# Thirty-two more bytes behind each of the six split-weight buffers of a two-layer hybrid trunk

## The chip, the core and the metric

The kernel runs on one core of one Trainium2 chip, in one launch. The metric is the device time of that launch in microseconds (us), the median of several runs. The core has a matrix engine (PE, with its weight loads listed apart as PEld), a vector engine (DVE), a scalar engine (ACT), GpSimd (POOL) and a queue engine (SP) that issues most of the transfers from device memory. Everything the engines read lies in the on-chip memory, which has 128 partitions; a tile takes the same bytes in every partition, and when this text gives an address, it is the byte within a partition.

## The reference

The program computes two layers of a decoder trunk on a 512 x 1024 sequence. Each layer is a half-weighted SwiGLU block, a mixer, and another half-weighted SwiGLU block, each on RMS-normalised input:

```python
x = x + 0.5 * swiglu(rmsnorm(x, g1), wg1, wu1, wd1)     # 1024 -> 2816 -> 1024
h = rmsnorm(x, gm)
z = h @ w_in                                            # columns go to three head groups
y = concat(s5_mixer(z...), hgrn2_mixer(z...), nsa_mixer(z...))
x = x + y @ w_out
x = x + 0.5 * swiglu(rmsnorm(x, g2), wg2, wu2, wd2)
```

A last normalisation closes the trunk. All inputs and weights are float32. Most of the arithmetic is in the dense products with `w_gate`, `w_up`, `w_down`, `w_in` and `w_out`.

## The kernel before

**Split products.** Activations are kept transposed (features on the partitions, the 512 tokens along the free axis). A float32 product is made of three products in the matrix engine's float32r type. Each operand is split into a rounded part and the rest: `whi` and `wlo` for the weights, and two halves each of `xs` (normalised input), `hb` (the hidden layer of the SwiGLU block) and `y` (mixer outputs) for the activations. `mm3` (lines 222 to 226) issues the three: L224 is `whi` by the rounded activation, L225 `whi` by the rest, L226 `wlo` by the rounded activation. In each of them a 128 x 128 block of weights is loaded and 512 token columns are streamed past it.

**The weights' way.** `wraw` (line 205) lets SP fetch up to 1024 columns of weights into one of four raw buffers. `wsplit` (line 212) takes one buffer named `whi` and one named `wlo` from pool `wp`, lets ACT round the raw weights into `whi` (L218), and lets DVE subtract to get `wlo` (L219). The pool has three buffers for each of the two names, so six in all. `dense_x` (line 228) uses a set for one output tile with eight 128-wide blocks; `ffn` (line 268) uses sets of 6 and 5 blocks for the down projection; `wout` (line 1353) uses sets of 4 blocks. `dense_tok` (line 1231, matmuls at L1250 to L1252) turns the roles round: there `xs` is loaded as the weight and 256 or 280 columns of `whi` or `wlo` are streamed. With 280 columns the slices of one buffer begin at columns 0, 280 and 560, which is byte 0, 1120 and 2240, or 0, 96 and 192 bytes past a multiple of 512.

**The order.** In the SwiGLU blocks the order is a plain loop, with small parameter work (`params`, line 378 on) woven in between. In the mixer a cooperative scheduler (`Weave`, line 38) interleaves generators for the dense projections and for the three head groups by weights and claimed costs that are written in the code. No address plays a part in either.

**Addresses.** The pools are opened in the constructor in a fixed order: `res`, `sm`, `al`, `big`, `wp`, and tiles are laid out in the order of their first use. `al` holds one unused tile of `ALIGN` = 192 bytes, behind which `x` begins at byte 24576, `xs` at 40960 and the raw weights at 73728, all multiples of 512. In the built program `whi` stands at 94208, 98304 and 102400, `wlo` at 106496, 110592 and 114688, each 4096 bytes long. Behind them stand `sq` (118784) and `rbc` (122880), and then the pools that come and go: the SwiGLU blocks' (`hb` at 129024, `ft`, `ft2`), the mixer's pool `mp` of 46 equal tiles of 2048 bytes from 126976 on, and the parameter pools. Tiles of the parameter pools do not begin at multiples of 512: `shm` and `Rs`, used by the matmuls of L703 and L704, begin 192 bytes past one in one layer and 480 past one in the other, and so do `cbw` and `cbt` of L717.

Of the kernel before, what the change touches and what calls it, by code (L numbers as in the profile page):

```python
# [11 lines left out]
F32R = mybir.dt.float32r  # L12
# [50 lines left out]
class Trunk:  # L63
# [147 lines left out]

    def wsplit(self, w, n, parts=1):
        nc = self.nc
        h = self.wp.tile([128, 1024], F32R, tag="whi", name="whi")
        lo = self.wp.tile([128, 1024], F32R, tag="wlo", name="wlo")
        for i in range(parts):
            sl = slice(i * n // parts, (i + 1) * n // parts)
            nc.scalar.copy(h[:, sl], w[:, sl])  # L218
            self.mark = nc.vector.tensor_tensor(lo[:, sl], w[:, sl], h[:, sl].bitcast(F32), op=OP.subtract)  # L219
        return h, lo  # L220
# [1277 lines left out]
```

## Time and profile before

| | |
|---|---|
| median of 3 runs | 2116.76 us (2115.8 to 2119.16) |
| the profiled execution, own time | 2116.3 us |
| its span, first to last instruction | 2114.5 us |
| PE busy | 2091.4 us, 99% of the span, 11192 matmuls |
| PEld busy (overlaps PE) | 1695.1 us, 80% |
| DVE busy | 1188.1 us, 56% |
| ACT busy | 786.7 us, 37% |
| POOL busy | 82.8 us, 4% |
| granted TensorE clock, mean | 0.996 of full speed |
| moved by DMA | 209.11 MB, 99 GB/s over the span |

The busy time of an engine is the time in which at least one of its instructions is shown as running. Matmuls are pipelined, so that one is shown for longer than it holds up the next: the pace of a stream of them is read from the distance between their starts. A group of instructions shows its busy time, the mean duration of one, and behind the second bar how long its engine was idle before it and what ended most of that. The chain of work that ended last is followed back from the last instruction, at each step to what released it.

### The profile page before, as it was taken

The page shows a single profiled execution, that of the slowest core. Times are in us where ns is not written, and L with a number is a line of the kernel's source. Part 1 is how long each engine was busy: PE and PEld are TensorE (multiplying, and loading weights), DVE is VectorE, ACT ScalarE, POOL GpSimd, SP SyncE. Part 2 cuts the span into 40 slices and gives each one's busy share as a digit, 9 for nine tenths or more (in the row PEclk, how much of TensorE's full clock was granted, in tenths as well). Part 3 has the DMA queues.
Part 4 walks back from the last instruction along what each step waited for, and adds up shares of the span by engine and source line. Part 5 has one row for each costly group of instructions (what it writes and reads, how often), then busy time and mean ns, then how long its engine had stood idle before and what let it go on. Part 6 is the DMA issues. An engine that isn't in the chain of part 4 may idle for free.

```text
span 2114.5 us, 28943 instructions
## 1 busy us (share of the span) xinstructions
PE 2091.4 (99%) x11192; PEld 1695.1 (80%) x11192; DVE 1188.1 (56%) x2653; ACT 786.7 (37%) x1455; POOL 82.8 (4%) x153
## 2 busy tenths in 40 slices
PE   8999999999999999999999999999999999999997
PEld 7888888877767888888888888888777678888886
DVE  7864545676765874543544343456777664334435
ACT  5322223445565432232332222243455663222321
POOL 1000000111000100000000000001100000000000
PEclk9999999999999999999999999999999999999999
DMA  5334433433101433432333233234321023333322
GB/s 193 112 104 128 138 127 104 139 113 101 51 16 43 149 117 95 150 97 81 109 100 94 83 114 100 75 115 138 110 75 51 26 80 90 87 93 113 97 82 68
DMA packets 69753, 209.11 MB, mean 99 GB/s; under 512 B 9272, under 2 KB 11912, under 8 KB 69616
## 3 DMA queue, kind: packets, MB, share of 16 engines
q1 hardware_dynamic: 58192, 172.19, 27.1%
q0 software_dynamic: 11280, 35.05, 4.8%
q8 instruction: 88, 1.44, 0.3%
q14 instruction: 49, 0.40, 0.1%
q10 hardware_dynamic: 144, 0.03, 0.0%
HBM read 194.63 MB, written 15.22 MB: 99 GB/s over the span
## 4 chain that ended last, share of the span: by engine, by line
PE 98%; DVE 1%; issue 0%; DMA 0%; ACT 0%; SPq 0%; POOL 0%; DVEq 0%; POOLq 0%
PE pd L224 28%; PE pd L226 27%; PE pd L225 27%; PE pno L1198 2%; PE ppt L1182 2%; PE psS L1159 2%; PE psS L1156 1%; PE plv L875 1%; PE pd L1250 1%; PE pd L1251 1%; PE pd L1252 1%; PE psc L1095 1%; PE pho L945 0%; PE pno L1201 0%; PE pY L784 0%
## 5 line engine op out<-in xcount | busy, mean ns | idle before, releaser
L218 ACT CAST whi<-wraw 128x1024 fp32r<-128x1024 f32 (+5 forms) x377 | 345.4, 917 | 1017.1 <-PE pd L225 703.6
L224 PE MATMUL pd<-xs,whi 128*128 128x512 f32 x1664 | 657.8, 395 | 6.7 <-ACT whi L218 6.1
L226 PE MATMUL pd<-xs,wlo 128*128 128x512 f32 x1664 | 652.2, 392 | 0.0
L225 PE MATMUL pd<-xs,whi 128*128 128x512 f32 x1664 | 650.8, 391 | 0.0
L219 DVE TENSOR_TENSOR wlo<-wraw,whi 128x1024 fp32r<-128x1024 f32 (+5 forms) x377 | 397.0, 1055 | 144.7 <-ACT whi L218 136.1
L224 PEld LDWEIGHTS pd<-xs,whi 128*128 128x128 f32 x1664 | 313.7, 188 | 76.1 <-ACT whi L218 6.1
L226 PEld LDWEIGHTS pd<-xs,wlo 128*128 128x128 f32 x1664 | 313.3, 188 | 66.6 <-issue 0.4
L225 PEld LDWEIGHTS pd<-xs,whi 128*128 128x128 f32 x1664 | 313.6, 188 | 64.1 <-DVE xs L164 1.0
L224 PE MATMUL pd<-hb,whi 128*128 128x512 f32 x682 | 265.8, 390 | 0.0
L226 PE MATMUL pd<-hb,wlo 128*128 128x512 f32 x682 | 265.4, 389 | 0.0
L225 PE MATMUL pd<-hb,whi 128*128 128x512 f32 x682 | 265.4, 389 | 0.0
L293 DVE TENSOR_TENSOR ft<-ft,pd 128x512 f32<-128x512 f32 x88 | 60.5, 687 | 247.5 <-PE pd L226 247.1
L287 DVE TENSOR_TENSOR ft<-pd,rbc 128x512 f32<-128x512 f32 x88 | 60.7, 690 | 189.0 <-PE pd L226 189.0
L226 PEld LDWEIGHTS pd<-hb,wlo 128*128 128x128 f32 x682 | 128.0, 188 | 26.8
L224 PEld LDWEIGHTS pd<-hb,whi 128*128 128x128 f32 x682 | 128.0, 188 | 26.3
L225 PEld LDWEIGHTS pd<-hb,whi 128*128 128x128 f32 x682 | 128.0, 188 | 26.3
L312 DVE TENSOR_TENSOR ft<-pd,r 128x512 f32<-128x512 f32 x62 | 42.9, 692 | 109.3 <-PE pd L226 109.1
L1166 ACT ACTIVATE P<-P,mx 128x128 f32<-128x128 f32 (+3 forms) x128 | 71.7, 561 | 51.9 <-DVE mx L1162 50.5
L1162 DVE CUSTOM_DVE_ANT_0 P<-Tb,psS 128x128 f32<-128x128 f32 (+3 forms) x128 | 60.7, 485 | 49.5 <-PE psS L1159 48.9
L295 DVE TENSOR_TENSOR hb<-ft,hb 128x512 fp32r<-128x512 f32 x88 | 60.3, 685 | 0.0
L288 ACT ACTIVATE ft<-ft 128x512 f32<-128x512 f32 x88 | 55.1, 627 | 13.1 <-DVE ft L287 12.8
L294 ACT CAST hb<-ft 128x512 fp32r<-128x512 f32 x88 | 54.8, 622 | 13.7 <-DVE ft L293 11.8
(388 smaller groups left out, 2158.3 us busy)
## 6 DMA issues: line engine op xcount, KB each, us to landing
wraw<-in_gu SPq DMA_DIRECT2D x175, 512.0 KB, 3.6
wraw<-in_dn SPq DMA_DIRECT2D x64, 384.0 KB, 3.1
wraw<-in_dn SPq DMA_DIRECT2D x64, 320.0 KB, 2.8
wraw<-in_win SPq DMA_DIRECT2D x32, 512.0 KB, 3.5
w<-sp POOLq DMA_DIRECT2D x32, 256.0 KB, 5.8
wraw<-in_wo SPq DMA_DIRECT2D x32, 256.0 KB, 2.6
Tb<-tbl POOLq DMA_DIRECT2D x16, 256.0 KB, 3.6
tbl<-ext POOLq DMA_DIRECT2D x1, 2560.0 KB, 19.7
```

The lines of the kernel that those rows point to most:

```text
L218: nc.scalar.copy(h[:, sl], w[:, sl])
L219: self.mark = nc.vector.tensor_tensor(lo[:, sl], w[:, sl], h[:, sl].bitcast(F32), op=OP.subtract)
L224: nc.tensor.matmul(ps, wh, xh, start=first, stop=False)
L225: nc.tensor.matmul(ps, wh, xl, start=False, stop=False)
L226: nc.tensor.matmul(ps, wl, xh, start=False, stop=last)
L287: nc.vector.tensor_tensor(t[:], pg[:], rbc[:], op=OP.mult)
L288: nc.scalar.activation(t[:], t[:], AF.Silu)
L293: nc.vector.tensor_tensor(t2[:], t[:], pu[:], op=OP.mult)
L294: nc.scalar.copy(hb[:, 0, f], t2[:])
L295: nc.vector.tensor_tensor(hb[:, 1, f], t2[:], hb[:, 0, f].bitcast(F32), op=OP.subtract)
L1162: v.tensor_tensor_reduce(p[:, :n], T[g][2 * hp + e][:, L - n:], ps[e][:, :n], 1.0, 1e29, OP.add, OP.min, mx[:, 2 * e + b:2 * e + b + 1])
L1166: nc.scalar.activation(P[j][:, :n], P[j][:, :n], AF.Exp, bias=mx[:, j:j + 1], scale=-1.0, accum_out=sm_[:, j:j + 1])
```

## The change

Both tiles of `wsplit` are declared with 1032 columns where they had 1024. The added eight columns (32 bytes) are never read or written. A blank line is added too, so that every line from 214 on has a number higher by one in the changed kernel (L218 becomes L219, L224 becomes L225).

```diff
     def wsplit(self, w, n, parts=1):
         nc = self.nc
-        h = self.wp.tile([128, 1024], F32R, tag="whi", name="whi")
-        lo = self.wp.tile([128, 1024], F32R, tag="wlo", name="wlo")
+
+        h = self.wp.tile([128, 1024 + 8], F32R, tag="whi", name="whi")
+        lo = self.wp.tile([128, 1024 + 8], F32R, tag="wlo", name="wlo")
```

In the built program the six buffers then begin at 94208, 98336, 102464 (`whi`) and 106592, 110720, 114848 (`wlo`), that is 0, 32, 64, 96, 128 and 160 bytes past a multiple of 512. Everything that is laid out behind them moves up by 6 x 32 = 192 bytes: `sq`, `rbc`, `r05`, `hb`, `ft`, `ft2`, all tiles of the mixer's pool and of the parameter pools. `x`, `xs`, the raw weights, `acc`, the pools `res` and `sm`, and all of the matrix engine's output banks stay where they were. The instructions of every engine, their order, their operands' names and shapes, and what each waits for are the same in both programs.

## Rows read from the trace of the kernel before

**Rows 1.** The page: busy time by engine, granted clock by slice, the group of casts.

```profile
PE 2091.4 (99%) x11192; PEld 1695.1 (80%) x11192; DVE 1188.1 (56%) x2653; ACT 786.7 (37%) x1455; POOL 82.8 (4%) x153
...
PEclk9999999999999999999999999999999999999999
...
L218 ACT CAST whi<-wraw 128x1024 fp32r<-128x1024 f32 (+5 forms) x377 | 345.4, 917 | 1017.1 <-PE pd L225 703.6
```

**Rows 2.** The chain that ended last, whole span: shares by engine and by line.

```profile
PE 98%; DVE 1%; issue 0%; DMA 0%; ACT 0%; SPq 0%; POOL 0%; DVEq 0%; POOLq 0%
```

**Rows 3.** Waits of PE: engine, line, waited for: us in total, times, longest.

```profile
PE pd L224 <- ACT whi L218: 6.1, 1, 6.1
PE pbc L196 <- DVE rsy L115: 3.5, 1, 3.5
...
PE pD L759 <- DMA U<-s5u: 0.4, 1, 0.4
```

**Rows 4.** Groups by line and shape, matmuls with split weights: xcount | busy, mean ns.

```profile
L224 PE MATMUL pd<-xs,whi 128*128 128x512 f32 x1664 | 657.8, 395 | 6.7 <-ACT whi L218 6.1 <-ACT xs L163 0.6
...
L224 PE MATMUL pd<-hb,whi 128*128 128x512 f32 x682 | 265.8, 390 | 0.0
...
L224 PE MATMUL pd<-y,whi 128*128 128x512 f32 x128 | 53.7, 422 | 0.2
```

**Rows 5.** Timeline of PE, down projection: start us, us, instruction.

```profile
371.94 0.39 PE L224 MATMUL pd<-hb,whi 128*128 128x512 f32 x1
...
376.02 0.39 PE L224 MATMUL pd<-hb,whi 128*128 128x512 f32 x1
```

**Rows 6.** Groups by line and shape: `wlo` streamed, 280 and 256 columns.

```profile
L1252 PE MATMUL pd<-wlo,xs 128*128 128x280 f32 x64 | 18.7, 292 | 0.0
L1252 PE MATMUL pd<-wlo,xs 128*128 128x256 f32 x64 | 18.1, 283 | 0.0
```

**Rows 7.** Timeline of PE, L1250 to L1252: slices at 0, 96, 192 and 0.

```profile
501.34 0.29 PE L1250 MATMUL pd<-whi,xs 128*128 128x280 f32 x1
...
501.72 0.29 PE L1250 MATMUL pd<-whi,xs 128*128 128x280 f32 x1
...
502.11 0.29 PE L1250 MATMUL pd<-whi,xs 128*128 128x280 f32 x1
...
502.50 0.29 PE L1250 MATMUL pd<-whi,xs 128*128 128x280 f32 x1
...
502.88 0.95 PE L955 MATMUL phn<-hsel,hsq 128*128 128x2 f32 x8
```

**Rows 8.** Line L703, weights `shm`, stream `Rs`: duration ns min/median/max, first and last start.

```profile
L703 PEld LDWEIGHTS ptt<-Rs,shm x16: 187/188/192, 196.3 to 845.0; 128*128 128x128 f32 x16
L703 PE MATMUL ptt<-Rs,shm x16: 279/280/283, 196.5 to 845.1; 128*128 128x256 f32 x16
```

**Rows 9.** Groups by line and shape: weight loads of `whi`, ACT's cast, DVE's subtraction.

```profile
L224 PEld LDWEIGHTS pd<-xs,whi 128*128 128x128 f32 x1664 | 313.7, 188 | 76.1 <-ACT whi L218 6.1 <-issue 3.4 <-ACT xs L163 1.2
...
L219 DVE TENSOR_TENSOR wlo<-wraw,whi 128x1024 fp32r<-128x1024 f32 x211 | 257.7, 1223 | 56.6 <-ACT whi L218 48.3
...
L218 ACT CAST whi<-wraw 128x512 fp32r<-128x512 f32 x32 | 19.9, 623 | 21.7 <-PE pd L225 21.5
```

**Rows 10.** Lines L717 (DVE) and L656 (ACT), parameter tiles: duration ns min/median/max.

```profile
L717 DVE TENSOR_TENSOR cbt<-cbw,cbp x4: 1220/1226/1226, 225.2 to 865.9; 128x1024 f32<-128x1024 f32 x4
...
L656 ACT CAST shm<-shf x4: 604/612/621, 20.2 to 704.1; 128x512 fp32r<-128x512 f32 x4
```

**Rows 11.** DMA issues: operation, xcount, KB each, median us to landing.

```profile
wraw<-in_gu SPq DMA_DIRECT2D x175, 512.0 KB, 3.6
...
cbw<-in_cw POOLq DMA_DIRECT2D x4, 512.0 KB, 3.7
```

**Rows 12.** The chain that ended last, 415 to 430 us: start us, us, what.

```profile
420.07 3.84 issue
423.93 3.40 DMA U<-s5u
427.47 1.97 PE pD L759 x16
```

## The prediction

> **What bounds the kernel now.** I read the page first. The matrix engine is busy for 2091.4 of 2114.5 us and its granted clock is nine tenths or more in all forty slices [rows 1]. The reader is to see that no second engine is near: the vector engine stands at 56%, the scalar engine at 37%. The chain that ended last says the same in another way: 98% of the span is PE work that follows PE work [rows 2]. Then the waits of PE: the longest are 6.1 us once at the start and 3.5 us once [rows 3]. So there is almost no wait that a change elsewhere could shorten, and only two things can move the time by more than a few microseconds: the pace of the matmuls themselves, or a new wait.
>
> Then the groups by line and shape [rows 4]. The matmuls on split weights with 512 columns are 1664 + 682 + 128 to a line, and `mm3` has three lines, so 3 x 2474 = 7422 of them. The mean of 390 to 422 ns in the row is the time one is shown for, not its price, since they overlap. The price is in the timeline of a down projection: 18 steps from 371.94 to 376.02 us, 4.08 us, so 226.7 ns each [rows 5]. 7422 x 226.7 ns = 1683 us, four fifths of the span. This is the number to hold on to: a nanosecond on each of these matmuls is 7.4 us, 0.35% of the time, while about 0.2% (4.2 us) is what a measurement of this kernel can tell from no change.
>
> **The change part by part.** No instruction is added, removed or moved, no operand grows and no wait changes; the added bytes have no reader. What changes is addresses. Five of the six split-weight buffers start 32 to 160 bytes past a multiple of 512, and all that lies behind them (`hb`, the mixer's and parameter tiles, `rbc`, `sq`) starts 192 bytes later. So each term is an operation that costs what it did before, unless its price depends on where an operand begins. The trace has such operands, and each term is a comparison.
>
> *Weights loaded from an odd place.* Five sixths of 7422 = 6185 matmuls now load their 128 x 128 block from a moved buffer. The nearest row is L703: its weights `shm` begin 192 bytes past a multiple of 512 in one layer and 480 in the other, which is a start of 32 past a multiple of 64 too. Their loads take 187/188/192 ns [rows 8], against a mean of 188 ns for `whi` at its present place [rows 9]. Term: 0.
>
> *Columns streamed from an odd place.* This concerns `hb` (3 x 682), `y` (3 x 128) and the streamed `whi` and `wlo` of L1250 to L1252. In L1252 the slices of 280 columns begin 0, 96 and 192 past a multiple of 512, those of 256 columns at 0. The groups show 292 and 283 ns [rows 6]. Twenty-four columns more at the granted 2.4 GHz are 10 ns, so 293 is what 280 columns would take with no penalty, and the row is 1 ns under that. The timeline of one such stretch is finer: three matmuls each on slices at 0, 96, 192 and 0 take 0.38, 0.39, 0.39 and 0.38 us [rows 7]. L703 again has both operands off at once: 280 ns against 283 for the same 256 columns [rows 8, 6]. Term: 0.
>
> *The bounds of these two.* The extremes are -3 ns a matmul (280 against 283) and +3.3 ns (0.02 us over six matmuls, which is also what rounding can do). On 6185 matmuls that is -18.6 and +20.4 us. I take 0: the weight loads show no difference at all, and the other rows lie on both sides of it within their rounding.
>
> *Making the split weights.* ACT writes `whi`, DVE reads it and writes `wlo`. The nearest rows are L717, two inputs and an output of 1024 columns at 192 or 480 past a multiple of 512: 1220/1226/1226 ns against a mean of 1223 in L219; and L656, a cast into float32r at such places: 604/612/621 ns against 623 [rows 9, 10]. Term: 0. If they were some nanoseconds slower, the cover is the second and third buffer of each name, and engines that are busy for 56% and 37% of the span; without that cover a set would be late by those nanoseconds, 377 sets in all [rows 1], so 10 ns each would be 3.8 us.
>
> *Transfers.* The fetches of raw weights and of `x` land where they did, so SP's queue sees nothing. GpSimd's transfers into and out of the moved tiles are the ones to cost. At present `cbw`, off by 192 or 480, lands its 512 KB in a median of 3.7 us and the raw weights, at multiples of 512, in 3.6 [rows 11]; the bounds are 0 and 3% of a transfer. One of these transfers lies on the chain, `U<-s5u` with 3.40 us [rows 12], and even there PE itself waits only 0.4 us [rows 3]. Term: 0, at most 0.1 us.
> The Trainium skill's DMA: Bandwidth & Descriptors (How a descriptor splits into AXI transactions) speaks against this change: a descriptor that does not start at a multiple of 256 bytes begins with a transaction from the boundary below, whose first bytes are thrown away. By that rule I estimate nine transactions instead of eight for a row of 2048 bytes; on the 3.40 us that is 0.4 us, in both layers 0.9 us, and the sum would be 2117.2 instead of 2116.3. No row here shows such a price: 3.7 against 3.6 us is 3%, where one transaction in eight would be 12%.
>
> **Sum.** 2116.3 us (the profiled execution) + 0 + 0 + 0 + 0 = 2116.3 us. That execution is 0.5 us under the median of the three runs, 2116.76, which is no difference.
>
> **The rivals.**
> *Slower, by the matrix engine's reads.* If a start off a multiple of 64 or 512 costs something only in the dense stream, where a load and a stream of 512 columns run at once for hundreds of microseconds, the short bursts of L703 and L1252 would not show it. The nearest price is the spread of the weight loads, 188 to 192 ns [rows 8]: 4 ns on 6185 matmuls is 24.7 us, so 2141 us. It would decide from 0.7 ns a matmul on (4.2 us over 6185). For it: nothing in the trace has a 512-column stream at an odd place. Against it: in rows 7 load and stream also overlap, with the same matmuls, and show nothing. Chance 0.14, with most of it below the full price.
> *Faster, by ending a collision.* At 2.4 GHz 512 columns alone take 213.3 ns, and a step takes 226.7. If the 13.4 ns were paid because weights and stream now begin at the same place within 512 bytes, the staggered buffers would save up to 7422 x 13.4 ns = 99 us and the time would be 2017 us. Against it: the slices at 96 and 192, which differ from the place of the loaded `xs`, keep the pace of those at 0 [rows 7]. A partial version, other engines' accesses that slow the stream now and no longer then, has little to win: the timeline steps at an even 226.7 while the others work. Chance 0.09 for both, 0.03 for more than 1%.
> *A late set of weights.* A wait of PE for `whi` at the start of a tile, in place of none now, by slower casts: 377 sets by 10 ns, 3.8 us, so 2120 us. It stays inside no change, and its chance is in the forecast's.
> *The change does not do what it says.* The built program has the addresses that the change names, and an unread pad that moved nothing would give 2116.3 as well; it can't be told from the forecast by the time.
>
> **How the numbers follow.** The forecast has 0.77, of which the late sets take a few hundredths: within 0.2% is 2112 to 2121 us. Slower by more has 0.14, faster by more 0.09. The range keeps the forecast's whole band, and reaches into the slower case as far as half its unknown price, about 1.7 ns a matmul, 2127 us; on the faster side, whose evidence is weaker, a microsecond beyond the band, 2111 us. The full bounds of the unknown prices, -18.6 and +20.4 us, would be 2098 and 2137; the outer halves have together less than 2 in 10.
>
> **What the changed profile would show.** Right: the down projection still steps at 226.7 ns although `hb` and the weights both moved; weight loads still at 188 ns, for all six buffers alike; the subtraction of 1024 columns at 1223 and the cast of 512 at 623 ns; PE busy within 4 us of 2091.4; no new wait among PE's. Wrong: any step other than 226.7 ns in the dense stretches, above all one that comes and goes with the buffer in use (0, 32, 64 past), or one in the `hb` stretches alone, whose stream moved, and not in the `xs` stretches, whose stream did not. If the time moves with the pace unchanged, the cause must be a new wait, most likely in one of the two mixers, where the head groups are interleaved.

## The result, and the profile after

The changed kernel takes 2152.01 us (median of 4 runs, 2151.77 to 2152.53), the kernel before 2116.86 us in the same session; the ratio is 1.0165 with a 95% interval of 1.0147 to 1.0183. It is 35 us slower, where no change was forecast. The instructions and their order are the same, so the time must be in how long they hold each other up.

The page of the changed kernel, against [rows 1], and its waits of PE, against [rows 3] (engine, line, waited for: us in total, times, longest):

```profile
span 2150.0 us, 28943 instructions
...
PE 2126.2 (99%) x11192; PEld 1694.2 (79%) x11192; DVE 1188.1 (55%) x2653; ACT 785.9 (37%) x1455; POOL 82.9 (4%) x153
...
PEclk9999999999999999999999999999999999999998
...
PE pd L225 <- ACT whi L219: 6.3, 2, 6.2
PE pbc L196 <- DVE rsy L115: 3.5, 1, 3.5
...
PE pD L760 <- DMA U<-s5u: 0.7, 1, 0.7
```

PE's busy time grew by 34.8 us and the span by 35.5. The other engines' busy times are the old ones to within 1 us, the waits to within 0.3 us, and the mean granted clock is 0.996 in both. So the loss is inside PE's own stream. The groups of the changed kernel, by line and shape (xcount | busy, mean ns), answer to [rows 4], [rows 6] and [rows 9]:

```profile
L225 PE MATMUL pd<-xs,whi 128*128 128x512 f32 x1664 | 666.9, 401 | 7.1 <-ACT whi L219 6.3 <-ACT xs L163 0.8
...
L225 PEld LDWEIGHTS pd<-xs,whi 128*128 128x128 f32 x1664 | 313.5, 188 | 84.1 <-ACT whi L219 6.8 <-issue 3.4 <-ACT xs L163 1.8
...
L225 PE MATMUL pd<-hb,whi 128*128 128x512 f32 x682 | 269.7, 395 | 0.0
...
L220 DVE TENSOR_TENSOR wlo<-wraw,whi 128x1024 fp32r<-128x1024 f32 x211 | 257.7, 1223 | 57.7 <-ACT whi L219 49.4
...
L225 PE MATMUL pd<-y,whi 128*128 128x512 f32 x128 | 54.0, 425 | 0.2
...
L219 ACT CAST whi<-wraw 128x512 fp32r<-128x512 f32 x32 | 19.9, 623 | 22.4 <-PE pd L226 21.9
```

A weight load still lasts 188 ns, the subtraction 1223 and the cast 623. Only the matmuls are shown for longer, by 3 to 6 ns in the mean, and in the stage that streams `xs` as well as in the stages that stream the moved `hb` and `y`. The timeline of the same 18 steps of the down projection, against [rows 5]:

```profile
380.28 0.39 PE L225 MATMUL pd<-hb,whi 128*128 128x512 f32 x1
...
384.45 0.40 PE L225 MATMUL pd<-hb,whi 128*128 128x512 f32 x1
```

18 steps take 4.17 us now, 231.7 ns each, where they took 226.7. A stage that streams `xs`, whose place did not change, shows the same. These are the first matmuls of four output tiles in a row, 24 steps apart, in the timeline of the kernel before, and then the same four in the changed one, where the tiles use the buffers at 0, 64, 32 and 0 past a multiple of 512:

```profile
287.62 0.39 PE L224 MATMUL pd<-xs,whi 128*128 128x512 f32 x1
...
293.06 0.39 PE L224 MATMUL pd<-xs,whi 128*128 128x512 f32 x1
...
298.50 0.39 PE L224 MATMUL pd<-xs,whi 128*128 128x512 f32 x1
...
303.94 0.39 PE L224 MATMUL pd<-xs,whi 128*128 128x512 f32 x1
```

```profile
293.99 0.39 PE L225 MATMUL pd<-xs,whi 128*128 128x512 f32 x1
...
299.56 0.39 PE L225 MATMUL pd<-xs,whi 128*128 128x512 f32 x1
...
305.13 0.40 PE L225 MATMUL pd<-xs,whi 128*128 128x512 f32 x1
...
310.69 0.39 PE L225 MATMUL pd<-xs,whi 128*128 128x512 f32 x1
```

5.44 us a tile before; 5.57, 5.57 and 5.56 after. The first of these tiles is made with a `whi` that has not moved at all, for an `xs` that has not moved either, and it loses as much as the others; only its `wlo`, which serves every third matmul, has moved (to 96). That is the first hint that no operand is slow by itself.

The whole sum: from the starts in the trace, about 7060 of the matmuls on split weights are followed directly by another one (steps of 300 ns and more, which hold other work or a wait, left out). Their mean step is 227.1 ns before and 232.0 after; 7060 x 4.87 ns = 34 us of the 35.5. The mixers hardly take part: the same matmul starts 8.7 us later at the beginning of the first mixer (around 400 us) and 9.9 us later at its end (around 697 us), 26.2 us later at the beginning of the second and 27.4 us at its end. There the dense matmuls are interleaved with others, and those on `y` had a mean step of 229.3 ns already before.

### The profile page after: what moved, and what is told of

Read it like the earlier page. It is cut to its first block, busy times and chain, and to the rows that moved or that the text cites. A ratio compares the mean times of both kernels' runs of the same rounds, so it can differ in the third digit from the quotient of the medians.

```text
span 2150.0 us, 28943 instructions
## 1 busy us (share of the span) xinstructions
PE 2126.2 (99%) x11192; PEld 1694.2 (79%) x11192; DVE 1188.1 (55%) x2653; ACT 785.9 (37%) x1455; POOL 82.9 (4%) x153
## 4 chain that ended last, share of the span: by engine, by line
PE 98%; DVE 1%; DMA 1%; issue 0%; SPq 0%; ACT 0%; POOL 0%; DVEq 0%; POOLq 0%
PE pd L225 28%; PE pd L227 27%; PE pd L226 27%; PE pno L1199 2%; PE ppt L1183 2%; PE psS L1160 2%; PE psS L1157 1%; PE plv L876 1%; PE pd L1251 1%; PE pd L1252 1%; PE pd L1253 1%; PE psc L1096 1%; PE pho L946 0%; PE pno L1202 0%; DMA x<-in_x 0%
## 5 line engine op out<-in xcount | busy, mean ns | idle before, releaser
L219 ACT CAST whi<-wraw 128x1024 fp32r<-128x1024 f32 (+5 forms) x377 | 344.4, 914 | 1065.3 <-PE pd L226 752.2
L225 PE MATMUL pd<-xs,whi 128*128 128x512 f32 x1664 | 666.9, 401 | 7.1 <-ACT whi L219 6.3
L226 PE MATMUL pd<-xs,whi 128*128 128x512 f32 x1664 | 657.0, 395 | 0.0
L225 PEld LDWEIGHTS pd<-xs,whi 128*128 128x128 f32 x1664 | 313.5, 188 | 84.1 <-ACT whi L219 6.8
L225 PE MATMUL pd<-hb,whi 128*128 128x512 f32 x682 | 269.7, 395 | 0.0
L226 PE MATMUL pd<-hb,whi 128*128 128x512 f32 x682 | 268.5, 394 | 0.0
L225 PEld LDWEIGHTS pd<-hb,whi 128*128 128x128 f32 x682 | 128.2, 188 | 29.4
```

The lines of the kernel that those rows point to most:

```text
L225: nc.tensor.matmul(ps, wh, xh, start=first, stop=False)
L226: nc.tensor.matmul(ps, wh, xl, start=False, stop=False)
```

## The experiments

In all of them only the addresses are changed, by the sizes of unused tiles. Where the padding needs room, the pool keeps one `acc` buffer instead of two (`bufs=1`), and in one case one `rbc`; the runs e3 and e11 show that this costs nothing, and the waits of PE add up to 15.8 to 17.3 us in every run, 16.0 before. The diffs leave out the lines that make room. "Distance" below is the start of the loaded weight block minus the start of the streamed columns, modulo 256; why 256, the fifth run shows. Blocks lie 512 bytes apart and streams 2048, so that within one set of weights the distance is constant. A step is the time from one matmul's start to the next one's. Lines are some rows higher or lower in each kernel's own file.

The theories at the start. **Same place:** the even step needs loaded weights and streamed columns to begin at the same place. **Absolute:** a start off a multiple of 512 costs by itself. **Changing weights:** the step is lost where one weight block begins elsewhere than the one before.

**e1: only what lies behind the buffers moves.**

```diff
         lo = self.wp.tile([128, 1024], F32R, tag="wlo", name="wlo")
+        self.wp.tile([128, 48], F32, tag="tail", name="tail", bufs=1)
```

> The split weights stay at multiples of 512; only what lies behind them (hb, y, rbc, sq) moves by 192 bytes. Same-place theory (the even step of 226.7 ns needs the loaded weights and the streamed columns to begin at the same place within 512 bytes): the stages that stream hb and y lose it, 2046 + 384 matmuls by about 5 ns, so 2127 to 2130 us, and the stages that stream xs keep 226.7 ns. Absolute theory (a start off a multiple of 512 costs by itself): the same 2127 to 2130 us. Changing-weights theory (the step is lost because one weight block and the next begin at different places): 2117 us, all stages at 226.7 ns.

Measured: 2131.15 us, ratio 1.0067 (1.0044 to 1.009). The timeline has an `xs` tile and 18 steps of the down projection:

```profile
295.12 0.39 PE L225 MATMUL pd<-xs,whi 128*128 128x512 f32 x1
...
300.56 0.39 PE L225 MATMUL pd<-xs,whi 128*128 128x512 f32 x1
...
375.52 0.39 PE L225 MATMUL pd<-hb,whi 128*128 128x512 f32 x1
...
379.72 0.39 PE L225 MATMUL pd<-hb,whi 128*128 128x512 f32 x1
```

The `xs` tile takes 5.44 us as before, and the 18 steps on `hb` take 4.20 us, 233.3 ns each. No weight block moved here, so changing weights falls as the sole cause. The loss is a little over what was expected, because the step grew by 6.6 ns and not by 5.

**e2: only the buffers are staggered**; a tail brings `hb` and the rest back to multiples of 512.

```diff
-        h = self.wp.tile([128, 1024], F32R, tag="whi", name="whi")
-        lo = self.wp.tile([128, 1024], F32R, tag="wlo", name="wlo")
+        h = self.wp.tile([128, 1024 + 8], F32R, tag="whi", name="whi")
+        lo = self.wp.tile([128, 1024 + 8], F32R, tag="wlo", name="wlo")
+        self.wp.tile([128, 80], F32, tag="tail", name="tail", bufs=1)
```

> The six buffers are staggered as in the change, and a tail of 320 bytes puts hb and all the rest back on multiples of 512 (room for it from one accumulator buffer less). Same-place theory: nearly all dense matmuls still off, about 2150 us. Changing-weights theory: 2150 us. Absolute theory: only the matmuls whose weights start off a multiple of 512 pay, 2145 us, and those with the one buffer that stayed at 0 step at 226.7 ns.

Measured: 2152.99 us, ratio 1.0172 (1.0142 to 1.0201). The stagger alone makes the whole loss; once it is there, moving `hb` as well adds nothing. The steps of the `xs` stages on the `whi` at 0 average 232.5 ns, on the two moved ones 232.2 and 232.5. The absolute theory wanted 226.7 there and does not fit.

**e3: 512 bytes of padding each.**

```diff
+        h = self.wp.tile([128, 1024 + 128], F32R, tag="whi", name="whi")
+        lo = self.wp.tile([128, 1024 + 128], F32R, tag="wlo", name="wlo")
```

> Each buffer gets 512 bytes more instead of 32, so that all still begin at multiples of 512 (room from one accumulator and one row-factor buffer less). All three theories: 2117 us. If it is slow, the cause is the spacing of the buffers or the smaller pools and not the place within 512 bytes.

Measured: 2116.92 us, ratio 1.0002 (0.999 to 1.0013). Neither the gap between the buffers nor the smaller pools matter.

**e4: everything 32 bytes further on.**

```diff
-    ALIGN = 192
+    ALIGN = 224
```

> The unused tile ahead of x gets 32 bytes more, so that x, xs, the split weights, hb and all the rest begin 32 bytes past a multiple of 512, all alike. Same-place and changing-weights theories: 2117 us. Absolute theory: every dense matmul pays, 2150 us or more.

Measured: 2117.18 us, ratio 1.0001 (0.9989 to 1.0012), and the tiles take 5.44 us:

```profile
288.25 0.39 PE L224 MATMUL pd<-xs,whi 128*128 128x512 f32 x1
...
293.69 0.39 PE L224 MATMUL pd<-xs,whi 128*128 128x512 f32 x1
```

Weights and streams all begin 32 past a multiple of 512 and nothing is lost. The absolute theory falls here.

**e5: the three pairs at 64, 128 and 256.** The three buffers of each name become three names with one buffer each, taking turns, so that a gap can be put ahead of each pair.

```diff
-        h = self.wp.tile([128, 1024], F32R, tag="whi", name="whi")
-        lo = self.wp.tile([128, 1024], F32R, tag="wlo", name="wlo")
+        i = self.wi = (getattr(self, "wi", -1) + 1) % 3
+        gap = (64, 64, 128)[i]
+        if gap and not hasattr(self, "gap%d" % i):
+            setattr(self, "gap%d" % i, self.wp.tile([128, gap // 4], F32, tag="gap%d" % i, name="gap", bufs=1))
+        h = self.wp.tile([128, 1024], F32R, tag="whi%d" % i, name="whi", bufs=1)
+        lo = self.wp.tile([128, 1024], F32R, tag="wlo%d" % i, name="wlo", bufs=1)
+        if i == 2 and not hasattr(self, "tail"):
+            self.tail = self.wp.tile([128, 64], F32, tag="tail", name="tail", bufs=1)
```

> The three pairs (one whi, one wlo each) begin 64, 128 and 256 bytes past a multiple of 512, both of a pair alike; xs, hb and the rest at multiples of 512. Same-place theory, places counted within 512 bytes: every dense stage is off, about 2150 us. If places count within 256 bytes only, the pair at 256 keeps 226.7 ns once it has settled, a third of the loss is saved, about 2140 us; within 128 bytes two pairs keep it, about 2129 us; within 64 bytes all, 2117 us. Changing-weights theory (the loss comes from a weight block that begins elsewhere than the block before): only the change of pairs disturbs, every 12 to 24 matmuls, so under 2130 us.

Measured: 2141.55 us, ratio 1.0116 (1.0073 to 1.016). Three tiles in a row, with the pairs at 64, 128 and 256:

```profile
292.55 0.40 PE L230 MATMUL pd<-xs,whi 128*128 128x512 f32 x1
...
298.14 0.39 PE L230 MATMUL pd<-xs,whi 128*128 128x512 f32 x1
...
303.72 0.39 PE L230 MATMUL pd<-xs,whi 128*128 128x512 f32 x1
...
309.16 0.40 PE L230 MATMUL pd<-xs,whi 128*128 128x512 f32 x1
```

5.59, 5.58 and 5.44 us. The pair at 256 has the even 226.7 ns of a distance of 0: the place counts within 256 bytes. And it has it in every tile, between two tiles that have not; so the step is the set's own and does not need a long run-up: in the mean of the `xs` stages the very first step after the change of pair is 227.6 ns. The pair at 64 steps by 235 and 231 ns in turn from the beginning of its tile to the end, although ACT and DVE write a next set in only some 2 us of each tile. So the step follows the set that PE reads, not the writing beside it.

**e6: all six buffers at 32, `xs` and `hb` at 0.**

```diff
+        self.wp.tile([128, 8], F32, tag="pre", name="pre", bufs=1)
         h = self.wp.tile([128, 1024], F32R, tag="whi", name="whi")
         lo = self.wp.tile([128, 1024], F32R, tag="wlo", name="wlo")
+        self.wp.tile([128, 120], F32, tag="tail", name="tail", bufs=1)
```

> All six buffers begin 32 bytes past a multiple of 512, alike; xs, hb and the rest at multiples of 512. Same-place theory: no dense stage settles, all steps at 231 to 234 ns, 2150 us. Changing-weights theory: no weight block differs from the one before, so 2117 us with 226.7 ns.

Measured: 2159.31 us, ratio 1.02 (1.0156 to 1.0244), slower than the change itself. Every tile takes the same:

```profile
295.35 0.40 PE L226 MATMUL pd<-xs,whi 128*128 128x512 f32 x1
...
300.95 0.40 PE L226 MATMUL pd<-xs,whi 128*128 128x512 f32 x1
```

5.60 us, 233.3 ns a step. Here all weight blocks begin alike, and the changing-weights theory falls for good: it is the distance between weights and stream that costs; this is e4 without the shift of the streams.

**e7: pairs at 96, 192 and 384** (as e5, with other gaps).

> The three pairs at 96, 192 and 384 bytes past a multiple of 512. Same-place theory within 512 bytes: 2150 us with all three pairs at 231 to 234 ns. Within 128 bytes: the pair at 384 settles to 226.7 ns, about 2140 us; within 64 bytes two of three do, about 2129 us. If some distance between weights and stream is better than none, its pair shows a step under 226.7 ns, down to 213.3 (512 columns at 2.4 GHz).

Measured: 2150.87 us, ratio 1.016 (1.0117 to 1.0204).

```profile
294.57 0.39 PE L230 MATMUL pd<-xs,whi 128*128 128x512 f32 x1
...
300.19 0.40 PE L230 MATMUL pd<-xs,whi 128*128 128x512 f32 x1
...
305.70 0.39 PE L230 MATMUL pd<-xs,whi 128*128 128x512 f32 x1
...
311.30 0.39 PE L230 MATMUL pd<-xs,whi 128*128 128x512 f32 x1
```

5.62 us at 96, 5.51 at 192, 5.60 at 384 (a distance of 128). A period of 128 or 64 is excluded, and each distance has a step of its own: in the mean of the `xs` stages 234.2, 229.4 and 232.7 ns.

**e8: `whi` at 0, `wlo` at 96.**

```diff
         h = self.wp.tile([128, 1024], F32R, tag="whi", name="whi")
+        self.wp.tile([128, 24], F32, tag="mid", name="mid", bufs=1)
         lo = self.wp.tile([128, 1024], F32R, tag="wlo", name="wlo")
+        self.wp.tile([128, 104], F32, tag="tail", name="tail", bufs=1)
```

> The three whi at multiples of 512 with xs and hb, the three wlo 96 bytes past one. Same-place theory, each matmul by itself: two thirds of the dense matmuls (L224, L225) keep 226.7 ns and one third (L226) pays 5 ns, about 2129 us. Same-place theory with a memory (the even step needs some ten matmuls in a row at one place): none settles, about 2150 us. Changing-weights theory: two of three weight loads begin elsewhere than the one before, about 2140 to 2150 us.

Measured: 2155.47 us, ratio 1.0182 (1.0138 to 1.0226). An `xs` tile takes 5.57 us:

```profile
295.10 0.39 PE L226 MATMUL pd<-xs,whi 128*128 128x512 f32 x1
...
300.67 0.40 PE L226 MATMUL pd<-xs,whi 128*128 128x512 f32 x1
```

In the `xs` stages the three lines average 233.2, 231.7 and 232.7 ns. One matmul in three at another distance takes the even step from the two at distance 0 too. Together with e5 and e7, where a new set has its own step from the first or second matmul on, this says that a step depends on the neighbours' distances, over a matmul or two, and not over ten as I had written. It is also the state of a third of the sets in the changed kernel (0 and 96).

**e9 and e10: finer distances.** As e5, with 256 bytes of room in each tile and a slice of it that starts at the wanted byte.

> The three pairs begin 160, 224 and 240 bytes past the stream's place within 256 bytes. Same-place theory with a period of 256 bytes and a step that is a fixed function of the distance: each pair has its own mean step in the xs and hb stages alike; from 229 ns at 192 falling back to 226.7 at 256, about 231, 228 and 227 ns, and 2125 to 2135 us. If only exactly the same place gives an even step and the row at 192 was chance, all three are at 232 to 234 ns and the time is 2150 us. A pair under 226.7 ns would show a place that beats both kernels.

> The three pairs begin 8, 16 and 248 (that is -8) bytes past the stream's place within 256 bytes. If the place counts in lines of 64 or 32 bytes, pairs 8 and 16 keep 226.7 ns and 248 does not; if every byte counts, the three steps lie between 226.7 and the 233.3 ns of a distance of 32, about 2125 to 2145 us; if only exact equality gives the even step, all at 232 to 234 ns and 2150 us.

Measured: 2148.89 us, ratio 1.0154 (1.0124 to 1.0183), and 2155.25 us, ratio 1.0184 (1.0154 to 1.0213). The tiles of e9, pairs at 160, 224 and 240:

```profile
293.14 0.39 PE L230 MATMUL pd<-xs,whi 128*128 128x512 f32 x1
...
298.74 0.40 PE L230 MATMUL pd<-xs,whi 128*128 128x512 f32 x1
...
304.34 0.40 PE L230 MATMUL pd<-xs,whi 128*128 128x512 f32 x1
...
309.81 0.39 PE L230 MATMUL pd<-xs,whi 128*128 128x512 f32 x1
```

5.60, 5.60 and 5.47 us. My expectation of a smooth way from 229 ns at 192 down to 226.7 at 256 was wrong: 224 is as bad as 32. The tiles of e10, pairs at 8, 16 and 248:

```profile
294.23 0.39 PE L230 MATMUL pd<-xs,whi 128*128 128x512 f32 x1
...
299.77 0.40 PE L230 MATMUL pd<-xs,whi 128*128 128x512 f32 x1
...
305.37 0.39 PE L230 MATMUL pd<-xs,whi 128*128 128x512 f32 x1
...
310.97 0.39 PE L230 MATMUL pd<-xs,whi 128*128 128x512 f32 x1
```

5.54, 5.60 and 5.60 us. No pair keeps 226.7 ns, so the place does not count in lines of 32 or 64 bytes; 8 bytes of distance already cost about half of the loss and 16 nearly all of it. That is the reading by which every byte counts, but its 2125 to 2145 us was too low, as the 2125 to 2135 us of e9 was. Mean steps in the `xs` stages, worked out from the starts in each trace as above:

| distance, bytes | 0 | 8 | 16 | 32 | 64 | 96 | 128 | 160 | 192 | 224 | 240 | 248 |
|---|---|---|---|---|---|---|---|---|---|---|---|---|
| step, ns | 227.1 | 230.6 | 233.0 | 233.3 | 233.4 | 234.2 | 232.5 | 233.5 | 229.4 | 233.4 | 227.7 | 233.3 |
| from | before | e10 | e10 | e6 | e5 | e7 | e5, e7 | e9 | e7 | e9 | e9 | e10 |

The `hb` stages repeat the `xs` row to within 1 ns at every distance, and e1, whose streams moved and not its weights (0 - 192, which is 64), has 233.4 on `hb`, the same as the pair at 64. No place tried is faster than 0, so there is no version here that beats both kernels.

**e11: the change with 256 bytes instead of 32.**

```diff
+        h = self.wp.tile([128, 1024 + 64], F32R, tag="whi", name="whi")
+        lo = self.wp.tile([128, 1024 + 64], F32R, tag="wlo", name="wlo")
```

> The change with 256 bytes of padding instead of 32 (room from one accumulator buffer less): the buffers lie at 0 and 256 past a multiple of 512, all else at multiples of 512. Same-place theory with a period of 256 bytes: 2117 us, 226.7 ns everywhere. If the period is 512 bytes and the pair at 256 in the earlier run was carried by its own even run only, the alternation of whi and wlo between 0 and 256 breaks the step: about 2150 us.

Measured: 2116.65 us, ratio 0.9996 (0.9984 to 1.0007). With pads in units of the period the change costs nothing.

## Why the prediction was wrong

*What bounds the kernel:* right. PE's stream sets the time, and the number to hold on to was named: a nanosecond on each dense matmul is 7.4 us. It moved by 4.9.

*The making of the split weights:* right, 1223 and 623 ns as before, and no new wait.

*Weights loaded, and columns streamed, from an odd place, both costed at 0:* these two steps failed; together they measured 4.9 ns in the mean step of the dense stream, 34 of the 35.5 us. The working took the price of an operand to be its own, to be read from other operands at odd places. It belongs to the pair: e4 moves weights and streams together and loses nothing, e6 moves the weights alone and loses 42 us.

The rows could not show it, for two reasons. In L703 weights and stream begin at 192 and 192, or 480 and 480, a distance of 0, which is exactly the case that e4 shows to be free [rows 8]. And its streams have 256 columns, those of rows 7 have 280: at these lengths the runs show no loss of that size even where the distance is not 0. In e6 no slice of 280 columns begins where the loaded `xs` does, and the mean step is 128.9 ns against 128.8 before. The streams of 256 columns even went the other way: their mean step, from the starts in the traces, is 119.9 ns before, 117.6 in the changed kernel and 116.7 in e6. The group of the changed kernel that answers to [rows 6] shows the same sign:

```profile
L1253 PE MATMUL pd<-wlo,xs 128*128 128x256 f32 x64 | 18.0, 280 | 0.0
```

280 ns where it was 283. Why the length of the stream decides the sign was not tried. I had also read the 188 ns of a weight load as if it carried the price; it stayed at 188 while the step grew.

*The count* of five sixths, 6185 matmuls, is off by itself: `whi` is loaded for two of the three matmuls, so the one unmoved buffer serves two ninths of them and the moved ones serve 5773. This changes no conclusion, since the sets with the unmoved buffer lose as well.

*The bounds* of -3 and +3.3 ns came from the same rows, the first from durations shown, which the working itself had set aside as no price. The measured 4.9 in the mean, up to 7 at a distance of 96, lay outside.

*The rival "slower, by the matrix engine's reads"* had the right engine, the right stages and the right objection (nothing in the trace streams 512 columns at an odd place), with 2141 us and a chance of 0.14. Its price and its condition were off: it took 4 ns from the spread of the weight loads, and it charged moved buffers only, while the unmoved one pays the same beside a moved `wlo`. I should have let its own objection weigh more: a row that has no such stream is no evidence against it.

*The rival "faster, by ending a collision":* wrong by the runs, which went the other way. Of the 13.4 ns that a step takes above 512 columns' 213.3, no distance tried gives any back.

*Transfers:* small, as said, though PE's wait for `U<-s5u` rose from 0.4 to 0.7 us, over the 0.1 allowed. On the chain that transfer takes 3.64 us, where it took 3.40 before [rows 12]; the estimate by the descriptor rule of the Trainium skill's DMA: Bandwidth & Descriptors (How a descriptor splits into AXI transactions) was 0.4 us more. Its medians are 3.7 us in the changed kernel, in e1 and in e4, where the tile moved, and 3.5 to 3.9 in the runs where it did not, so the traces neither bear the rule out nor refute it.

*What would show it wrong* was named rightly ("any step other than 226.7 ns in the dense stretches"): the changed kernel steps at 231.7 ns there. The step does not come and go with the buffer in use, though, nor with the moved stream alone.

What stays open is why. The runs settle which condition costs how much; what inside the chip makes a load and a stream that begin 32 bytes apart slower than two that begin together was not tried.

## What to carry to other kernels

Where a dense stream of float32r matmuls with 512 columns sets the time, keep the start of the loaded weights and the start of the streamed columns equal modulo 256 bytes, for all buffers that take turns, and pad in units of 256 (shorter streams did not lose here); an innocent pad can take 2% without changing one instruction. When a price may depend on addresses, look for rows with the same pair of operands in the same kind of stream, of the same length, and ask of each row whether it could have shown the effect. And read the pace from the starts: neither the weight loads' duration nor any wait showed this loss.

## What the runs showed of the hardware that I had not expected

- A stream of float32r matmuls, 128 x 128 weights by 512 columns, steps at 226.7 ns when weights and stream begin at the same place within 256 bytes, and at 227.7 to 234.2 ns at eleven other distances. The dependence is not smooth: 240 bytes 227.7 ns, 248 bytes 233.3 ns.
- A common shift of weights and streams costs nothing, as far as tried: all at 32 past a multiple of 512 gives 2117.18 us.
- With 256 columns the sign is the other way: the mean step of L1250 to L1252 fell from 119.9 ns to 117.6 in the changed kernel (its L1251 to L1253) and to 116.7 in e6. With 280 columns it stayed at 128.8 to 128.9 in the same runs.
- The Trainium skill's SBUF — State Buffer (Who interferes with whom) gives the matrix engine two independent read ports, one for the streamed operand and one for the weights. The runs differ from what I would make of that: the step depends on where the two begin with respect to each other, by up to 7 ns in 227.
